# Token-major Fourier branch on half the spectrum, and modulation bursts issued 3000 instead of 400 places ahead

## The chip, the core and the metric

The kernel runs on one core of a Trainium2 chip. A core has TensorE (PE, matmuls into PSUM, 8 banks of 128 x 512 float32), VectorE (DVE), ScalarE (ACT), GpSimd (POOL) and SyncE (SP), which issues most of the transfers. The metric is the device time of one execution in microseconds; less is better. The time before is the median of 3 runs.

## What is computed

Two layers of a diffusion backbone over 256 latent and 256 context tokens, width 1024. A layer modulates and normalises its input, projects it, runs three mixers beside each other (latent attention "MLA", grouped attention "GQA", and a Fourier mixer), merges them with sigmoid gates, projects, and ends in a gated ConvFFN. The second layer computes only the latent tokens beyond the keys and values. The parts that the change touches are these:

```
mod = silu_c @ w_mod + b_mod                  # 1024 x 6144, for the latents and for the context
h = rms_norm(x, g) * (1 + scale) + shift      # scale and shift are parts of mod
f = (h @ w_in)[..., FOUR_START:GATE_START]    # 512 columns: 4 groups of 128

def fourier_mix(f):                           # per sample of 256 tokens
    z = fftn(f.reshape(b, l, 4, 128), axes=(tokens, channels of a group), norm="ortho")
    return real(z).reshape(b, l, 512)
y = ... + g_four * (fourier_mix(f) @ w_four)
```

For real input, the real part of the two-dimensional transform is C_tok f C_ch - S_tok f S_ch, with C and S the cosine and sine matrices over tokens and over channels. The order of the two transforms is free. The cosine part is even and the sine part odd in the token frequency, so that the frequencies 129 to 255 follow from 1 to 127.

## The kernel before

All matrix products are done as three matmuls (`mm3`, lines 104 to 106): each operand is split (`split`, lines 118 to 126) into a rounded high part on ScalarE and the rest on VectorE, and high x high, high x low and low x high are summed in one PSUM bank. Weights arrive by `wchunk` (line 89 issues the transfer on SP's queue) in pieces of 128 x 1024, three buffers deep, and are split too.

The kernel is written in an ordinary order: modulation of layer 0, norm, keys and values, GQA queries, the Fourier branch, GQA heads with gate and branch projections between them as fillers, latents, MLA heads with fillers, output projection, norm, FFN; then layer 1. A planner fixes each engine's order when the program is built: among the instructions that its own timeline shows ready it takes the one with the lowest rank, and the rank is the place in the ordinary order. `tc.high_priority(n)` moves the rank n places ahead. PSUM banks have names: "mm", "s" and "pt" have two buffers each, "o" and "tk" one each. On-chip tiles with one tag share its buffers in the same way.

Fourier branch (lines 554 to 600). `TQ` is 512 tokens in layer 0 (two samples, NS = 2) and 256 in layer 1. In each of two rounds `c` of 256 channels, the projection is made channel-major (`fp`: weights as the stationary operand, tokens moving, TQ columns); its result `f`, channels on partitions, is the stationary operand of the channel transform (`Y`: cosine and sine side by side, 256 columns for each of two groups), and `Y`, tokens on partitions, is that of the sequence transform (`Z`: four matmul triples for each group and sample, two token tiles x cosine and sine, 256 columns). Each of `fp`, `Y` and `Z` is split on its way to the next step. `load_dft` (line 1059) loads and splits five tables of 128 x 256; three of them hold tiles of the tag "pr", which the attention's softmax also uses.

Modulation bursts (`mod_burst`, line 235). A layer's 6 blocks of 1024 modulation columns are computed in bursts, a quarter of the reduction at a time: two transfers of 512 KB into the two buffers "mraw", 8 matmuls at line 254 that each use a strip of 32 columns of the array (the profile counts 16), and the sum into `row`. The fourth burst of a block ends with `turn`, two transposes in the same bank. Most bursts use the bank "tk". The bursts are placed as fillers between heads and FFN steps; their matmuls alone are moved ahead by MOD_AHEAD:

```
with tc.high_priority(MOD_AHEAD):
    for i in (1, 0):
        k = 2 * q + i
        for g in range(4):
            nc.tensor.matmul(ps[32 * g:32 * g + 32, :256], ...)
```

Of the kernel before, what the change touches and what calls it, by code (L numbers as in the profile page):

```python
# [8 lines left out]
F32 = mybir.dt.float32  # L9
F32R = mybir.dt.float32r  # L10
# [5 lines left out]
P = 128  # L16
D = 1024
KD = D // P
# [7 lines left out]
FOUR_START = 1440  # L26
# [4 lines left out]
RAWBUFS = 3  # L31
WBUFS = 3
RSQRT_MAGIC = 0x5F3759DF
MOD_AHEAD = 400


@with_exitstack
def hybrid_kernel(ctx: ExitStack, tc: tile.TileContext, a: dict, out: bass.AP):
    nc = tc.nc
# [5 lines left out]
    S = ctx.enter_context(tc.tile_pool(name="S", bufs=1))  # L45
# [8 lines left out]
    def pm(name, tag="mm"):  # L54
        return psum.tile([P, 512], F32, tag=tag, name=name, bufs=BANKS[tag])

    def pair(tag, name, bufs=None):

        return S.tile([P, 2, 512], F32R, tag=tag, name=name, bufs=bufs)
# [20 lines left out]
    def wchunk(W, k0, nk, c0, ncol, name):  # L80

        npc = -(-nk * ncol // WMAX)
        kpp = -(-nk // npc)
        parts = []
        for i in range(0, nk, kpp):
            kn = min(nk - i, kpp)
            n = kn * ncol
            raw = wpool.tile([P, WMAX], F32, tag="raw", name=f"{name}_w{i}", bufs=RAWBUFS)
            ins = nc.sync.dma_start(
                out=raw[:, :n].rearrange("p (k c) -> p k c", k=kn),  # L90
                in_=W[(k0 + i) * P:(k0 + i + kn) * P, c0:c0 + ncol].rearrange("(k p) c -> p k c", p=P))
            hi = wpool.tile([P, WMAX], F32R, tag="whi", name=f"{name}_h{i}", bufs=WBUFS)
            lo = wpool.tile([P, WMAX], F32R, tag="wlo", name=f"{name}_l{i}", bufs=WBUFS)
            split(raw[:, :n], hi[:, :n], lo[:, :n])
            parts.append((hi, lo))

        def w(k, c, m):
            j, r = divmod(k, kpp)
            return tuple(t[:, r * ncol + c:r * ncol + c + m] for t in parts[j])
        w.last = ins.ins  # L100
        return w
# [13 lines left out]
    def split(src, hi, lo, scale=None, later=False):  # L115

        if scale is None:
            nc.scalar.copy(hi, src)  # L118
        else:
            nc.scalar.activation(hi, src, AF.Copy if isinstance(scale, float) else AF.Identity, scale=scale)  # L120

        def low():
            if scale is None:
                nc.vector.tensor_sub(lo, src, f(hi))  # L124
            else:
                nc.vector.scalar_tensor_tensor(lo, src, scale, f(hi), op0=ALU.mult, op1=ALU.subtract)
        if later:
            return low
        low()
# [238 lines left out]
    def fm_group(w, cols, nk, xs, T, evac, name, tag="mm", whole=None):  # L368


        if T * len(cols) <= 512 and nk <= KD:
            ps = pm(f"{name}_0", tag)
            pss = [ps[:, i * T:(i + 1) * T] for i in range(len(cols))]
            order = [(k, i) for i in range(len(cols)) for k in range(nk)]
        else:
            pss = [pm(f"{name}_{i}", tag[i] if isinstance(tag, tuple) else tag) for i in range(len(cols))]
            order = [(k, i) for k in range(nk) for i in range(len(cols))]
        for k, i in order:
            wh, wl = w(k, cols[i], P)
            mm3(pss[i][:, :T], wh, wl, xs[k][:, 0, :T], xs[k][:, 1, :T], k == 0, k == nk - 1)  # L380
        if whole and T * len(cols) <= 512:
            whole(ps[:, :T * len(cols)])
            return
        rest = [evac(i, pss[i][:, :T]) for i in range(len(cols))]
        for r in rest:
            if callable(r):
                r()
# [19 lines left out]
    def layer(l, p, modT, last, xT, mods, prep, wkvg=None, norm=None):  # L407
        n_ = f"L{l}"
        TQ = 256 if last else 512
        NTQ = TQ // P  # L410
# [143 lines left out]
        of_ = []  # L554
        with after("qg0"):
            dft = load_dft(l)
        for c in range(2):
            w = wchunk(w_in, 0, KD, FOUR_START + c * 256, 256, f"{n_}fo{c}")
            if last:
                ft = S.tile([P, 2, 2, TQ], F32R, tag=f"D{2 * c}", name=f"{n_}f{c}")  # L560
                fs = [ft[:, i] for i in range(2)]
            else:
                fs = [pair(f"D{2 * c + i}", f"{n_}f{c}{i}") for i in range(2)]
            fm_group(w, [0, P], KD, hs, TQ,
                     lambda i, ps: split(ps, fs[i][:, 0, :TQ], fs[i][:, 1, :TQ], later=True), f"{n_}fp{c}", "mm" if c == 0 else "o" if last else ("o", "tk"),
                     whole=lambda ps: split(ps.rearrange("p (i t) -> p i t", i=2), ft[:, :, 0, :], ft[:, :, 1, :]))
            Y = []
            for tt in range(NTQ):
                ps = pm(f"{n_}Y{c}{tt}", "s")
                ts = slice(tt * P, (tt + 1) * P)  # L570
                for i in range(2):
                    mm3(ps[:, i * 256:(i + 1) * 256], fs[i][:, 0, ts], fs[i][:, 1, ts],
                        dft[0][:, 0, :], dft[0][:, 1, :], True, True)
                y = pair(f"X{tt}", f"{n_}Y{c}{tt}")
                split(ps, y[:, 0, :], y[:, 1, :])
                Y.append(y)
            if last:
                zp = pm(f"{n_}Z{c}", "pt")
                zps = [zp[:, :TQ], zp[:, TQ:]]
            for i in range(2):  # L580
                ps = zps[i] if last else pm(f"{n_}Z{c}{i}", "pt")
                for s in range(NS):
                    n = 0
                    for t2 in range(2):
                        for cs in range(2):
                            y = Y[s * 2 + t2]
                            wsl = slice(i * 256 + cs * P, i * 256 + (cs + 1) * P)
                            q = 1 + t2 * 2 + cs
                            mm3(ps[:, s * 256:(s + 1) * 256], y[:, 0, wsl], y[:, 1, wsl],
                                dft[q][:, 0, :], dft[q][:, 1, :], n == 0, n == 3)  # L590
                            n += 1
                if not last:
                    o = pair(f"B{2 * c + i}", f"{n_}fo{c}{i}")
                    split(ps, o[:, 0, :], o[:, 1, :])
                    of_.append(o)
            if last:
                op = S.tile([P, 2, 2, TQ], F32R, tag=f"B{c}", name=f"{n_}fo{c}")
                split(zp.rearrange("p (i t) -> p i t", i=2), op[:, :, 0, :], op[:, :, 1, :])
                of_ += [op[:, 0], op[:, 1]]
        gF, bF = merge(2, "w_four", of_, True)  # L600

        def attend(scores, vl, o_dst, odd, nm):
# [456 lines left out]
    def load_dft(l):  # L1059

        d4 = S.tile([P, 2, 2, 256], F32R, tag="D4", name=f"dft{l}d")
        ts = [d4[:, 0], d4[:, 1]] + [S.tile([P, 2, 256], F32R, tag="pr", name=f"dft{l}{i}", bufs=3) for i in range(3)]
        for i, t in enumerate(ts):
            if i == 0:
                src = a["dft_d"]
            else:
                t2, cs = divmod(i - 1, 2)
                src = a["dft_s"][t2 * P:(t2 + 1) * P, cs * 256:(cs + 1) * 256]
            raw = S.tile([P, 256], F32, tag="ot", name=f"dft{l}r{i}", bufs=2)
            nc.sync.dma_start(out=raw, in_=src)  # L1070
            nc.scalar.copy(t[:, 0, :], raw)
            nc.vector.tensor_sub(t[:, 1, :], raw, f(d4)[:, i, 0, :] if i < 2 else f(t)[:, 0, :])
        return ts
# [35 lines left out]
def _tables():  # L1109
    import numpy as np  # L1110

    def rope(rot_dim):
        n_f = rot_dim // 4
        t = np.arange(SEQ)
        row, col = (t // 64).astype(np.float32), (t % 64).astype(np.float32)
        inv = (np.float32(10000.0) ** (-np.arange(n_f, dtype=np.float32) / np.float32(n_f))).astype(np.float32)
        ang = np.concatenate([row[:, None] * inv, col[:, None] * inv], axis=-1).astype(np.float32)
        c, s = np.cos(ang, dtype=np.float32), np.sin(ang, dtype=np.float32)
        return np.concatenate([c, c, -s, s], axis=-1)

    rope_tab = np.concatenate([rope(32), rope(64)], axis=-1).astype(np.float32)

    def dft(n):
        k = np.arange(n)
        ang = 2.0 * np.pi * ((k[:, None] * k[None, :]) % n) / n
        return np.cos(ang) / np.sqrt(n), np.sin(ang) / np.sqrt(n)

    cd, sd = dft(128)
    cs, ss = dft(SEQ)
    return {  # L1130
        "rope_tab": np.ascontiguousarray(rope_tab),
        "dft_d": np.concatenate([cd, sd], axis=1).astype(np.float32),
        "dft_s": np.concatenate([cs, -ss], axis=1).astype(np.float32),
    }


# [25 lines left out]
```

## Time and profile before

| | |
|---|---|
| median of 3 runs | 1423.36 us (1422.74 to 1425.29) |
| the profiled execution | 1422.24 us |
| its span, first to last instruction | 1420.40 us |
| PE busy | 1379.5 us |
| DVE, ACT, POOL busy | 892.4, 662.2, 332.9 us |

The profiled execution's time is 1.84 us longer than its span and 1.12 us shorter than the median. Matmuls are pipelined: the length shown for one contains the time until its result has left the array, so the pace is read from start to start and not from the length. A line of a helper (104, 118, 124) serves many places; there the tile's name says which.

### The profile page before, as it was taken

To read this page: it belongs to the slowest core of one execution; us is meant where nothing else is said; L and a number is where in the kernel's file an instruction comes from. 1 tells how busy PE (TensorE), PEld (TensorE's weight loads), DVE (VectorE), ACT (ScalarE), POOL (GpSimd) and SP (SyncE) were. 2 spreads that over 40 slices of the span, in tenths; PEclk is the share of its full clock that TensorE was granted. 3 is DMA by queue.
4 is the path that set the end of the run, shared out by engine and by line. 5 is a ranking of instruction groups with operands and counts; after the bars stand their busy time and mean duration, and the time that the engine had idled before them with its cause. 6 is when DMAs were issued, how large, how long until landed. Compare 5 with 4: busy or idle time off the path is not lost.

```text
span 1420.4 us, 23006 instructions
## 1 busy us (share of the span) xinstructions
PE 1379.5 (97%) x8801; PEld 1195.3 (84%) x8801; DVE 892.4 (63%) x1644; ACT 662.2 (47%) x1164; POOL 332.9 (23%) x399
## 2 busy tenths in 40 slices
PE   6999999999999999999999999999998998999998
PEld 4988888878888788878678888899977998899998
DVE  5575655666645666655326663677687766788853
ACT  4434545435554344444114442445564663566642
POOL 3211323364323311101000111121245332112200
PEclk9999999999999999999999999999999999999999
DMA  9733442143321745343343232363744555466663
GB/s 318 247 89 105 148 146 73 54 120 106 90 74 38 262 149 197 101 148 104 104 134 91 87 99 91 111 177 95 229 134 140 155 176 188 129 180 186 184 191 121
DMA packets 163064, 197.97 MB, mean 139 GB/s; under 512 B 7144, under 2 KB 149530, under 8 KB 162954
## 3 DMA queue, kind: packets, MB, share of 16 engines
q1 hardware_dynamic: 161952, 195.85, 44.5%
q0 software_dynamic: 864, 0.61, 0.4%
q8 instruction: 69, 1.13, 0.3%
q14 instruction: 41, 0.34, 0.1%
q10 hardware_dynamic: 138, 0.04, 0.0%
HBM read 192.28 MB, written 3.15 MB: 138 GB/s over the span
## 4 chain that ended last, share of the span: by engine, by line
PE 89%; DVE 5%; DMA 2%; POOL 1%; issue 1%; ACT 1%; SPq 1%; DVEq 0%; ACTq 0%; POOLq 0%
PE L0upp L104 6%; PE L0upp L105 6%; PE L0upp L106 6%; PE mod_ps L254 3%; PE L1upp L104 3%; PE L1upp L105 3%; PE L1upp L106 3%; PE L0dp L106 3%; PE L0dp L104 3%; PE L0dp L105 3%; PE L0gp L106 3%; PE L0gp L104 3%; PE L0gp L105 3%; PE L1dp L106 1%; PE L1dp L104 1%; PE L1dp L105 1%
## 5 line engine op out<-in xcount | busy, mean ns | idle before, releaser
L104 PE MATMUL L0upp<-L0n_h,L0up_h 128*128 128x512 f32 (+1 forms) x384 | 141.7, 373 | 1.1 <-ACT L0n_h L332 1.1
L105 PE MATMUL L0upp<-L0n_h,L0up_h 128*128 128x512 f32 (+1 forms) x384 | 141.9, 373 | 0.0
L106 PE MATMUL L0upp<-L0n_h,L0up_l 128*128 128x512 f32 (+1 forms) x384 | 140.0, 373 | 0.0
L984 POOL TENSOR_TENSOR L0sg<-L0sg,L0u 128x512 f32<-128x512 f32 x22 | 31.4, 1426 | 288.6 <-DVE L0u L961 274.9
L104 PE MATMUL L1upp<-L1n_h,L1up_h 128*128 128x256 f32 x352 | 96.5, 286 | 1.1 <-ACT L1n_h L332 1.1
L106 PE MATMUL L1upp<-L1n_h,L1up_l 128*128 128x256 f32 x352 | 97.0, 285 | 0.0
L105 PE MATMUL L1upp<-L1n_h,L1up_h 128*128 128x256 f32 x352 | 96.4, 285 | 0.0
L124 DVE TENSOR_TENSOR L0up_l<-L0up_w,L0up_h 128x1024 fp32r<-128x1024 f32 x44 | 58.8, 1337 | 53.7 <-ACT L0up_h L118 50.6
L104 PEld LDWEIGHTS L0upp<-L0n_h,L0up_h 128*128 128x128 f32 x384 | 71.8, 188 | 15.4 <-issue 1.6
L106 PEld LDWEIGHTS L0upp<-L0n_h,L0up_l 128*128 128x128 f32 x384 | 72.1, 188 | 13.6 <-issue 0.8
L105 PEld LDWEIGHTS L0upp<-L0n_h,L0up_h 128*128 128x128 f32 x384 | 72.0, 188 | 13.5 <-issue 0.8
L118 ACT CAST L0up_h<-L0up_w 128x1024 fp32r<-128x1024 f32 x44 | 46.3, 1053 | 72.2 <-PE L0upp L105 49.7
L104 PE MATMUL L0gp<-L0n_h,L0g_h 128*128 128x512 f32 x192 | 76.3, 397 | 0.0
L105 PE MATMUL L0gp<-L0n_h,L0g_h 128*128 128x512 f32 x192 | 75.5, 393 | 0.0
L106 PE MATMUL L0gp<-L0n_h,L0g_l 128*128 128x512 f32 x192 | 75.2, 396 | 0.1
L106 PE MATMUL L0dp<-L0act,L0dn_l 128*128 128x512 f32 (+1 forms) x196 | 72.7, 371 | 0.0
L104 PE MATMUL L0dp<-L0act,L0dn_h 128*128 128x512 f32 (+1 forms) x196 | 72.6, 370 | 0.0
L105 PE MATMUL L0dp<-L0act,L0dn_h 128*128 128x512 f32 (+1 forms) x196 | 72.5, 370 | 0.0
L104 PEld LDWEIGHTS L1upp<-L1n_h,L1up_h 128*128 128x128 f32 x352 | 66.9, 194 | 1.5 <-ACT L1n_h L332 1.5
L106 PEld LDWEIGHTS L1upp<-L1n_h,L1up_l 128*128 128x128 f32 x352 | 67.3, 194 | 0.0
L105 PEld LDWEIGHTS L1upp<-L1n_h,L1up_h 128*128 128x128 f32 x352 | 66.8, 194 | 0.0
L124 DVE TENSOR_TENSOR L1up_l<-L1up_w,L1up_h 128x1024 fp32r<-128x1024 f32 x44 | 54.2, 1231 | 18.6 <-ACT L1up_h L118 17.2
(1534 smaller groups left out, 4322.9 us busy)
## 6 DMA issues: line engine op xcount, KB each, us to landing
mod_w<-in_w_mod_dram SPq DMA_DIRECT2D x96, 512.0 KB, 5.0
L0up_w<-in_w_up_dram SPq DMA_DIRECT2D x44, 512.0 KB, 3.6
L1up_w<-in_w_up_dram SPq DMA_DIRECT2D x44, 512.0 KB, 4.3
L0g_w<-in_w_in_dram SPq DMA_DIRECT2D x24, 512.0 KB, 3.7
L1g_w<-in_w_in_dram SPq DMA_DIRECT2D x24, 512.0 KB, 4.0
L0dn_w<-in_w_down_dram SPq DMA_DIRECT2D x20, 512.0 KB, 3.5
L1dn_w<-in_w_down_dram SPq DMA_DIRECT2D x16, 512.0 KB, 3.5
L0wo_w<-in_w_o_dram SPq DMA_DIRECT2D x8, 512.0 KB, 7.0
```

What stands on the lines that cost most here:

```text
L104: nc.tensor.matmul(ps, lh, rh, start=start, stop=False)
L105: nc.tensor.matmul(ps, lh, rl, start=False, stop=False)
L106: last_mm[0] = nc.tensor.matmul(ps, ll, rh, start=False, stop=stop).ins
L118: nc.scalar.copy(hi, src)
L124: nc.vector.tensor_sub(lo, src, f(hi))
L254: nc.tensor.matmul(ps[32 * g:32 * g + 32, :256], cpad[:, 2 * k:2 * k + 32], raws[i][:, g * 256:(g + 1) * 256], start=i == 1, stop=i == 0, ...
L984: nc.gpsimd.tensor_mul(g[:, :TQ], g[:, :TQ], us[1][:, :TQ])
```

## The change

The Fourier branch is made token-major: the projection takes the tokens as the stationary operand and 512 channels as the moving one; its result, tokens on partitions, goes into the sequence transform first (`A`: 129 cosine and 127 sine frequencies side by side, 256 columns), and that into the channel transform, with the table as the stationary operand: `zc` (cosine, 2 x 130 columns) and `zs` (sine, 2 x 128). The frequencies 0 to 128 of `z` are the sum and 129 to 255 the difference, written in reverse order, of the two. Two of the five tables are gone. MOD_AHEAD goes from 400 to 3000.

```diff
-MOD_AHEAD = 400
+MOD_AHEAD = 3000
...
-        for c in range(2):
-            w = wchunk(w_in, 0, KD, FOUR_START + c * 256, 256, f"{n_}fo{c}")
...
-            fm_group(w, [0, P], KD, hs, TQ, ...)
-            Y = []
-            for tt in range(NTQ):
-                ps = pm(f"{n_}Y{c}{tt}", "s")
...
-            for i in range(2):
-                ps = zps[i] if last else pm(f"{n_}Z{c}{i}", "pt")
-                for s in range(NS):
...
+        w = wchunk(w_in, 0, KD, FOUR_START, 512, f"{n_}fo")
+        pss = [pm(f"{n_}fp{tt}", ("mm", "s")[tt // 2]) for tt in range(NTQ)]
+        for k0 in range(0, KD, 2):
+            for tt in range(NTQ):
+                ts = slice(tt * P, (tt + 1) * P)
+                for k in (k0, k0 + 1):
+                    wh, wl = w(k, 0, 512)
+                    mm3(pss[tt], hs[k][:, 0, ts], hs[k][:, 1, ts], wh, wl, k == 0, k == KD - 1)
+        ft = [pair(f"D{tt}", f"{n_}f{tt}") for tt in range(NTQ)]
+        for tt in range(NTQ):
+            split(pss[tt], ft[tt][:, 0, :], ft[tt][:, 1, :])
+
+        nb = 2 * NS
+        pss = [pm(f"{n_}A{b}", ("pt", "pt", "o", "tk")[b] if not last else "s") for b in range(nb)]
+        for s in range(NS):
+            for g in range(4):
+                b, hf = (g, s) if NS == 2 else divmod(g, 2)
+                gs = slice(g * P, (g + 1) * P)
+                for t2 in range(2):
+                    f_ = ft[s * 2 + t2]
+                    mm3(pss[b][:, hf * 256:(hf + 1) * 256], f_[:, 0, gs], f_[:, 1, gs],
+                        dft[1 + t2][:, 0, :], dft[1 + t2][:, 1, :], t2 == 0, t2 == 1)
+        As = [pair(f"X{b}", f"{n_}A{b}") for b in range(nb)]
+        for b in range(nb):
+            split(pss[b], As[b][:, 0, :], As[b][:, 1, :])
+        for b in range(nb):
+            ah, al = (As[b][:, i, :].rearrange("p (s k) -> p s k", s=2) for i in range(2))
+            zc = pm(f"{n_}Zc{b}", "mm" if not last else "pt")[:, :260].rearrange("p (s k) -> p s k", s=2)
+            zs = pm(f"{n_}Zs{b}", "s" if not last else ("o", "tk")[b])[:, :256].rearrange("p (s k) -> p s k", s=2)
+            mm3(zs, dft[0][:, 0, P:], dft[0][:, 1, P:], ah[:, :, P:], al[:, :, P:], True, True)
+            mm3(zc, dft[0][:, 0, :P], dft[0][:, 1, :P], ah[:, :, :130], al[:, :, :130], True, True)
+            zt = S.tile([P, 256], F32, tag="ot", name=f"{n_}zt{b}", bufs=2).rearrange("p (s k) -> p s k", s=2)
+            nc.scalar.copy(zt, zs)
+            z = S.tile([P, 512], F32, tag="pr", name=f"{n_}z{b}", bufs=3)
+            z3 = z.rearrange("p (s k) -> p s k", s=2)
+            nc.vector.tensor_add(z3[:, :, 1:P], zc[:, :, 1:P], zt[:, :, 1:])
+            nc.vector.tensor_sub(z3[:, :, 255:P:-1], zc[:, :, 1:P], zt[:, :, 1:])
+            nc.scalar.copy(z3[:, :, 0:P + 1:P], zc[:, :, 0:P + 1:P])
...
+                o = pair(f"B{b}", f"{n_}fo{b}")
+                split(z, o[:, 0, :], o[:, 1, :])
+                of_.append(o)
...
-        ts = [d4[:, 0], d4[:, 1]] + [S.tile([P, 2, 256], F32R, tag="pr", name=f"dft{l}{i}", bufs=3) for i in range(3)]
+        ts = [d4[:, 0], d4[:, 1], S.tile([P, 2, 256], F32R, tag="pr", name=f"dft{l}", bufs=3)]
...
-        "dft_s": np.concatenate([cs, -ss], axis=1).astype(np.float32),
+        "dft_s": np.concatenate([cs[:, :129], -ss[:, 1:128]], axis=1).astype(np.float32),
```

## Rows read from the trace of the kernel before

**Rows 1.** The page: busy time per engine, and the chain by engine.

```profile
PE 1379.5 (97%) x8801; PEld 1195.3 (84%) x8801; DVE 892.4 (63%) x1644; ACT 662.2 (47%) x1164; POOL 332.9 (23%) x399
...
PE 89%; DVE 5%; DMA 2%; POOL 1%; issue 1%; ACT 1%; SPq 1%; DVEq 0%; ACTq 0%; POOLq 0%
```

**Rows 2.** Windows: stretch, length, busy PE, PEld, DVE, ACT, POOL, clock, DMA.

```profile
71.00:117.00 46.00, 46.00 (x276) 41.10 (x275) 31.77 (x63) 17.39 (x27) 5.86 (x11) 1.00 0.28 81
941.00:975.00 34.00, 34.00 (x243) 31.99 (x242) 25.28 (x54) 16.18 (x24) 5.26 (x11) 1.00 0.46 130
1050.00:1090.00 40.00, 32.60 (x230) 28.65 (x229) 34.83 (x74) 22.23 (x41) 24.17 (x25) 0.99 0.55 163
```

**Rows 3.** Timeline of PE in layer 0's Fourier stage: start, length, instruction.

```profile
72.04 0.39 PE L106 MATMUL L0fp<-L0n_h,L0fo_l 128*128 128x512 f32 x1
...
85.64 0.39 PE L106 MATMUL L0fp<-L0n_h,L0fo_l 128*128 128x512 f32 x1
...
110.85 0.28 PE L104 MATMUL L0Z<-dft,L0Y 128*128 128x256 f32 x1
...
111.81 0.28 PE L106 MATMUL L0Z<-dft,L0Y 128*128 128x256 f32 x1
```

**Rows 4.** Windows by tile: L0fp, L0Y, L1fp, L1Y; busy PE (count), PEld, DVE, ACT.

```profile
66.00:125.00 59.00, 22.49 (x96) 17.76 (x96) 2.73 (x4) 2.34 (x4) 1.00 0.23 65
...
66.00:125.00 59.00, 18.70 (x144) 18.19 (x144) 5.34 (x8) 4.60 (x8) 1.00 0.23 65
...
935.00:980.00 45.00, 11.85 (x96) 11.66 (x96) 1.36 (x2) 1.17 (x2) 1.00 0.46 130
...
935.00:980.00 45.00, 9.50 (x72) 9.16 (x72) 2.67 (x4) 2.25 (x4) 1.00 0.46 130
```

**Rows 5.** Instructions by tile, L0Y and mod_ps: ns min/median/max, first and last start.

```profile
L118 ACT CAST L0Y<-L0Y x8: 587/588/591, 89.9 to 110.9; 128x512 fp32r<-128x512 f32 x8
L124 DVE TENSOR_TENSOR L0Y<-L0Y,L0Y x8: 680/691/693, 90.5 to 111.6; 128x512 fp32r<-128x512 f32 x8
...
L261 DVE TENSOR_TENSOR mod_row<-mod_row,mod_ps x30: 394/420/422, 132.2 to 1219.2; 128x256 f32<-128x256 f32 x30
...
L258 ACT COPY mod_row<-mod_ps x10: 353/372/390, 124.6 to 1215.9; 128x256 f32<-128x256 f32 x10
```

**Rows 6.** Timeline of PE around a modulation burst at 617 us.

```profile
617.05 0.39 PE L106 MATMUL L0upp<-L0n_h,L0up_l 128*128 128x512 f32 x1
617.37 1.07 PE L254 MATMUL mod_ps<-mod_w,cpad 128*32 128x256 f32 x16
...
618.71 0.40 PE L105 MATMUL L0upp<-L0n_h,L0up_h 128*128 128x512 f32 x1
```

**Rows 7.** Timeline of PE around two other bursts, 657 to 684 and 706 to 714 us.

```profile
657.21 0.39 PE L105 MATMUL L0upp<-L0n_h,L0up_h 128*128 128x512 f32 x1
...
658.42 0.39 PE L104 MATMUL L0upp<-L0n_h,L0up_h 128*128 128x512 f32 x1
...
676.58 0.39 PE L105 MATMUL L0dp<-L0act,L0dn_h 128*128 128x512 f32 x1
...
684.10 0.39 PE L106 MATMUL L0dp<-L0act,L0dn_l 128*128 128x512 f32 x1
...
705.87 0.39 PE L106 MATMUL L0dp<-L0act,L0dn_l 128*128 128x512 f32 x1
706.19 0.62 PE L254 MATMUL mod_ps<-mod_w,cpad 128*32 128x256 f32 x2
...
714.37 0.39 PE L105 MATMUL L0dp<-L0act,L0dn_h 128*128 128x512 f32 x1
```

**Rows 8.** Chain in order of time and SP's timeline: two bursts and the loads between.

```profile
122.90 1.00 PE mod_ps L254 x16
...
130.87 1.00 PE mod_ps L254 x16
...
123.53 0.81 SPq L248 DMA_DIRECT2D mod_w<-in_w_mod_dram  x2
```

More of the change, by code (lines that the diff above doesn't have):

```diff
@@ L559, in layer @@
             if last:
-                ft = S.tile([P, 2, 2, TQ], F32R, tag=f"D{2 * c}", name=f"{n_}f{c}")
-                fs = [ft[:, i] for i in range(2)]
-            else:
[L563 to L566, printed above, removed]
@@ L567, in layer @@
-            Y = []
-            for tt in range(NTQ):
-                ps = pm(f"{n_}Y{c}{tt}", "s")
-                ts = slice(tt * P, (tt + 1) * P)
-                for i in range(2):
[L572 to L579, printed above, removed]
@@ L580, in layer @@
-            for i in range(2):
-                ps = zps[i] if last else pm(f"{n_}Z{c}{i}", "pt")
-                for s in range(NS):
[L583 to L599, printed above, removed]
+                op = S.tile([P, 2, 2, TQ], F32R, tag=f"B{b}", name=f"{n_}fo{b}")
+                split(z3, op[:, :, 0, :], op[:, :, 1, :])
+                of_ += [op[:, 0], op[:, 1]]
+            else:
+                o = pair(f"B{b}", f"{n_}fo{b}")
+                split(z, o[:, 0, :], o[:, 1, :])
+                of_.append(o)
@@ L1066, in load_dft @@
             else:
-                t2, cs = divmod(i - 1, 2)
-                src = a["dft_s"][t2 * P:(t2 + 1) * P, cs * 256:(cs + 1) * 256]
+                src = a["dft_s"][(i - 1) * P:i * P, :]
             raw = S.tile([P, 256], F32, tag="ot", name=f"dft{l}r{i}", bufs=2)
```

## The prediction

> **What bounds the kernel now.** I read the page first: TensorE is busy 97% of the span, VectorE 63%, and 89% of the chain that ended last is TensorE time [rows 1]. 40.9 us of the 1420.4 us are without a matmul. So a microsecond of matmuls removed should be about a microsecond gained, unless the removed piece stood in a stage that waits for something else. I checked that by stretches [rows 2]: through both layers' Fourier stages TensorE is busy without a break (46.00 of 46, 34.00 of 34) while VectorE has room (31.77 and 25.28). In layer 1 a later stretch is different: from 1050 to 1090 TensorE does 32.60 of 40 and VectorE 34.83.
>
> Then the pace of the matmuls, from the starts in the timeline, since their shown lengths overlap [rows 3]: from 72.04 to 85.64 lie 60 starts of 512 columns, 0.2267 us each; from 110.85 to 111.81 lie 8 starts of 256 columns, 0.120 us each. Last, the modulation bursts, one by one [rows 5 to 7].
>
> **Change, part 1: Fourier matmuls.** The counts by tile [rows 4] agree with the code. Layer 0 now: 96 projection matmuls of 512 columns, and 144 of 256 that read or write Y (48 for the channel transform, 96 for the sequence transform). After: the projection is 8 k x 4 token tiles x 3 = 96 of 512 columns, the same; the sequence transform 2 samples x 4 groups x 2 token tiles x 3 = 48 of 256; the channel transform 4 tiles x 2 x 3 = 24 of 256 or 260. 144 become 72: 72 x 0.120 = 8.64 us less. 260 columns against 256 adds under 2% of 12 matmuls, nothing.
> Layer 1 now: 96 of 256 columns for the projection and 72 on Y, 168 x 0.120 = 20.16 us. After: 8 x 2 x 3 = 48 of 512, 24 and 12 of 256: 48 x 0.2267 + 36 x 0.120 = 15.20. 4.96 us less.
>
> **Part 2: what the other engines do.** A split of 512 columns takes 0.587 us on ScalarE and 0.690 on VectorE; 256 columns read from PSUM take VectorE 0.42 and ScalarE 0.37 [rows 5]. Layer 0 had 16 splits; it gets 12 splits and, for each of 4 tiles, an add, a subtract and two copies. VectorE: 16 x 0.690 = 11.0 becomes 12 x 0.690 + 8 x 0.42 = 11.6; ScalarE 9.4 becomes 8.5 to 10.0, as the two-column copy is near nothing or near 0.37. Layer 1: 8 splits (5.5) become 6 and 4 adds (5.8). The reversed write of the subtract has no row: below, the plain 0.42; above, I allow 0.69. Two of five DFT loads go in each layer, each with a split shorter than those rows. Together this is within 1 us of nothing on engines with room [rows 2], hidden by the matmuls; uncovered it appears in part 4. Weights arrive in pieces of the same size; a piece now feeds 12 matmuls of 512 columns in layer 1 (2.72 us) where it fed 24 of 256 (2.88): at most 4 x 0.16 = 0.6 us of waiting, I take none.
>
> **Part 3: the modulation bursts.** A burst is 8 matmuls (16 in the trace) on four 32-column strips. Issued in one piece it costs little: from the start at 617.05 to that at 618.71 are 1.66 us, of which two normal intervals are 0.45, so 1.21 us [rows 6]. Two of the 40 bursts are not in one piece: their pairs stand one by one between down-projection matmuls. The second takes 705.87 to 714.37 with 11 normal intervals (2.49): 8.50 - 2.49 = 6.01 us. The first has one pair at 657 (1.21 - 0.45 = 0.76) and seven from 676.58 to 684.10 (7.52 - 10 x 0.2267 = 5.25): 6.01 us again [rows 7]. One burst matmul and one ordinary matmul alternate: I read this as two runs of equal rank, the burst moved ahead by 400 and the ordinary order at that place, merged by the planner. Moved ahead by 3000 they would meet no equal: their data is not loaded that early, so they should go out in one piece when it is. 2 x (6.01 - 1.21) = 9.6 us less. Bounds: 0 if they stay threaded, 9.6. I take 9.6, as 38 of 40 bursts are in one piece.
> For those 38 I expect nothing. The first burst ends after 122.90, the load for the next is issued at 123.53 and its matmuls stand at 130.87 [rows 8]: buffers, loads and the one "tk" bank time them, not the rank. A burst's loads keep their ordinary place on SP's queue, behind the weights; if bursts run earlier, so do the loads that wait for their two buffers.
>
> **Part 4: new waits.** All four projection accumulators now close in the last weight piece, 6 x 0.2267 = 1.36 us apart, and the channel transform turns over two "mm" and two "s" banks for four tiles. After the sequence transform's last matmul, VectorE needs 0.587 + 0.690 for the last split and 0.84 for the first add and subtract: a bank is free at 2.12 us, while two tiles give TensorE 2 x 0.72 = 1.44. So 0.68 of waiting, then 0.12 and 0.84 for the next turns: 1.6 us. Behind these matmuls wait the gate group (same "mm" banks) and the first head's scores ("s"); the key transposes can fill. I take 2.0 in layer 0. In layer 1 the latent projection is ready and needs other banks by then: 0.5. Bounds: 0 below; above, every turn in series, 1.28 + 1.28 + 4 x 1.53 = 8.7 in layer 0 and 1.28 + 1.28 + 2 x 1.53 = 5.6 in layer 1, 14.3 together. I choose 2.5, near the lower end, because the same kinds of split ended 16 times in layer 0's stage without one gap [rows 2].
> The Trainium skill speaks against the change here: "Perfetto Trace Analysis", section "Matmuls", wants independent groups to rotate through different PSUM banks so that emptying one overlaps the next group. By that rule the turns would lie open and the saving would shrink by the 14.3; the full TensorE rows of that stage are against so much.
> Layer 1's stretch at 1050 to 1090 [rows 2] may swallow part of layer 1's gain, as VectorE's work before it does not shrink: 0 to 4.96; I take 1.5, since the matmuls that feed this stretch come earlier too.
>
> **Sum.** -8.64 - 4.96 - 9.60 + 2.5 + 1.5 = -19.2 us. The profiled execution took 1422.24 us (span 1420.40 and 1.84 around it): 1403.0. The median of the runs is 1.12 above it: 1404. With 0.2% (2.8 us) about what a measurement of this kernel can tell from no change, this is clearly faster.
>
> **Rivals.** (a) The bursts stay threaded, or thread elsewhere: -9.6 us is missing, 1414. For it: the planner's ranks aren't in the trace. Against: 38 whole bursts.
> (b) The turns of part 4 lie open, also by the skill's rule: 2.5 becomes 14.3, 1416. For it: two banks for four tiles. Against: gate and key work is at hand.
> (a) and (b) together: 9.6 + 11.8 of the 19.2 are gone; that ends at 1425.6, no change.
> (c) Slower: bursts so far ahead take the one "tk" bank, and the fourth burst of a block keeps it until its transposes, which keep their ordinary place. Heads that need "tk" for their transposes then wait for a gate group, 48 x 0.2267 = 10.9 us. Five blocks run beside attention; from two holds uncovered on (21.8) it is no gain, with three (32.6) 1437. Against it: burst and bank already alternate by data and buffers [rows 8]. For it: one bank, and the distance.
> (d) Better: no new wait, and fuller TensorE later; 23.2 or more less, below 1400.
>
> **How the numbers follow.** Chances: the forecast (1398 to 1409) 0.50, (a) 0.14, (b) 0.13, both 0.06, (c) 0.07, (d) 0.10. Faster by over 0.2%: 0.50 + 0.14 + 0.13 + 0.10 = 0.87; within: 0.06; slower: 0.07. The range 1396 to 1417 takes in the forecast, (a), (b) and half of (d), 0.82.
>
> **What the profile will show.** TensorE busy time lower by some 20 us; no mod_ps piece "x2" near 650 to 715; 72 matmuls of 256 columns in layer 0's Fourier stage, its TensorE gaps under 3 us; attention waits for "tk" not longer. I am wrong if TensorE gets new gaps of over 10 us in all, if bursts thread in other places, or if layer 1's end moves less than its start.

## The result, and the profile after

The median falls from 1423.98 us (1422.74 to 1425.29, 4 runs) to 1407.06 us (1404.73 to 1411.13, 4 runs): ratio 0.9884, 95% interval 0.9855 to 0.9913, that is 16.5 us less (12.4 to 20.6). The forecast was 1404, in a range of 1396 to 1417. The profiled execution after took 1404.73 us, its span is 1403.0, 17.4 below that of before. One execution on record, of a kernel of experiment 6, took 4798 us with each of its stretches 2.9 to 3.6 times as long, and no number here uses it.

The page after, busy time by engine and the chain; it answers to [rows 1]:

```profile
PE 1359.2 (97%) x8645; PEld 1180.0 (84%) x8645; DVE 889.1 (63%) x1646; ACT 660.0 (47%) x1166; POOL 336.2 (24%) x399
...
PE 89%; DVE 5%; DMA 2%; ACT 1%; POOL 1%; issue 1%; SPq 0%; DVEq 0%; ACTq 0%; POOLq 0%
```

TensorE does 20.3 us less and still bounds the kernel. A span cannot be judged by its length alone here. I cut it at instructions that every version has, and list the time from the first of one tile to the first of the next (A: L0fp to L0o, layer 0's Fourier branch and attention; B: L0upp to L1kvg, layer 0's FFN; C: L1fp to L1m0tk, the first key transposes of layer 1's latent heads; D: L1fp to L1o, of which C is the first part; the rest is what is left of the span, the same code in all versions but for the loads and splits of the DFT tables, two fewer in a layer with the new branch):

| profile | A | B | C | D | rest |
|---|---|---|---|---|---|
| before | 393.7 | 387.8 | 123.9 | 240.9 | 398.0 |
| after | 387.6 | 378.2 | 123.9 | 243.0 | 394.2 |
| difference | -6.1 | -9.6 | 0.0 | +2.1 | -3.8 |

So in this pair of profiles layer 0's Fourier branch gave 6.1 us, the bursts 9.6, layer 1's Fourier branch cost 2.1, and 3.8 came from the rest, where the change touches only the table loads. The experiments below show that of these the 9.6 repeats best, to within 0.6.

**The bursts.** TensorE's timeline after, the places of the two bursts of [rows 7]:

```profile
633.49 0.39 PE L105 MATMUL L0upp<-L0n_h,L0up_h 128*128 128x512 f32 x1
633.81 1.07 PE L254 MATMUL mod_ps<-mod_w,cpad 128*32 128x256 f32 x16
634.81 0.51 PE L106 MATMUL L0upp<-L0n_h,L0up_l 128*128 128x512 f32 x1
635.15 0.40 PE L104 MATMUL L0upp<-L0n_h,L0up_h 128*128 128x512 f32 x1
...
643.01 1.07 PE L254 MATMUL mod_ps<-mod_w,cpad 128*32 128x256 f32 x16
```

Both stand whole now, earlier than before and among the up-projection's matmuls. From 633.49 to 635.15 are 1.66 us, as in [rows 6].

**Layer 0's Fourier stage.** The counts of the tiles (one line of three for the projection, one of six for the sequence transform with its two tables, one of six for the channel transform, whose other three are L0Zs):

```profile
L104 PE MATMUL L0fp<-L0fo_h,L0n_h x32: 389/389/397, 73.5 to 94.6; 128*128 128x512 f32 x32
...
L104 PE MATMUL L0A<-dft,L0f x8: 283/283/284, 96.3 to 100.6; 128*128 128x256 f32 x8
...
L104 PE MATMUL L0Zc<-L0A,dft0d x4: 284/336/391, 101.1 to 107.4; 128*128 128x260 f32 x4
```

L0fp has 96 matmuls as before, and the 144 of 256 columns became 72. Windows of after: the layer-0 stage from the first L0fp to the first gate matmul, and in layer 1 from the first L1fp to the first gate matmul. Before, such stretches had no gap in layer 0 [rows 2] and 0.2 us in layer 1 (41.50 of 41.70).

```profile
73.50:107.90 34.40, 31.79 (x173) 27.41 (x173) 27.76 (x61) 14.37 (x27) 4.61 (x9) 1.00 0.33 92
925.30:965.10 39.80, 37.11 (x221) 32.57 (x219) 31.47 (x73) 20.46 (x33) 7.12 (x14) 1.00 0.44 124
```

Each now has 2.6 to 2.7 us without a matmul. In layer 0 it is one gap; TensorE's timeline and then ScalarE's at that place, after:

```profile
104.54 0.28 PE L106 MATMUL L0Zc<-L0A,dft0d 128*128 128x260 f32 x1
107.43 0.39 PE L104 MATMUL L0Zc<-L0A,dft0d 128*128 128x260 f32 x1 [2.61 <-ACT L0z L595]
```

```profile
104.84 0.58 ACT L798 CAST L0KG<-L0gk 64x512 fp32r<-64x512 f32 x1
105.42 0.58 ACT L799 CAST L0KG<-L0gk 64x512 fp32r<-64x512 f32 x1
106.01 0.58 ACT L798 CAST L0KG<-L0gk 64x512 fp32r<-64x512 f32 x1
106.60 0.58 ACT L799 CAST L0KG<-L0gk 64x512 fp32r<-64x512 f32 x1
107.21 0.17 ACT L595 COPY L0z<-L0Zc 128x4 f32<-128x4 f32 x1
```

The fourth tile's cosine matmuls need the "mm" bank of the second one. That bank's last reader is the two-column copy of line 595, 0.17 us long, and it stands on ScalarE behind four key copies of 0.58 us. The Trainium skill, "PSUM — Partial Sum Buffer", section "Engine vs sequencer instructions", calls ScalarE's and VectorE's queues strictly first in, first out; the trace agrees, the copy starts 0.03 us after the last key copy ends. VectorE's last read of that bank, the subtract of line 594, had ended at 104.5 us. The key copies empty the key transposes that stood at 103.61, the very filler that the prediction had counted on.

**Layer 1.** The waits of TensorE from 925 to 1017 us, after:

```profile
PE L1cq L104 <- DVE L1ck L126: 1.2, 1, 1.2
PE L1A L106 <- DVE L1f L124: 1.1, 1, 1.1
PE L1gp L104 <- DVE L1rkv_y L141: 0.4, 1, 0.4
```

The second is the turn from the projection to the sequence transform, which needs both token tiles split; the first is the latent projection, which comes earlier and now waits for VectorE. And then the first key transposes, before and after; for after also what stands ahead of them: the copies and squares of the keys, their sums (line 736), the first and the last of the nine steps of the root (lines 136 to 144) and the scaling (tiles L1ktok, L1SK and L1rk_y; shortest, median and longest in ns, first and last start):

```profile
L867 PE MATMUL L1m0tk<-ident,L1ktok x4: 270/314/315, 1065.3 to 1068.3; 128*96 128x128 f32 x4
```

```profile
L729 ACT COPY L1ktok<-L1ukv x8: 362/366/392, 1019.5 to 1037.2; 128x256 f32<-128x256 f32 x8
L734 POOL TENSOR_TENSOR L1kq<-L1ktok x8: 612/612/927, 1030.0 to 1038.5; 128x256 f32<-128x256 f32 x8
L736 DVE TENSOR_REDUCE L1SK<-L1kq x8: 399/402/420, 1031.2 to 1040.7; 128x4 f32<-128x256 f32 x8
...
L136 DVE TENSOR_SCALAR L1rk_y<-L1SK x1: 180/180/180, 1041.4 to 1041.4; 128x32 int32<-128x32 int32 x1
...
L144 DVE SCALAR_TENSOR_TENSOR L1rk_y<-L1rk_t,L1rk_y x1: 964/964/964, 1047.0 to 1047.0; 128x32 f32<-128x32 f32 x1
L746 DVE TENSOR_TENSOR L1ktok<-L1ktok,L1rk_y x4: 693/1097/1105, 1048.0 to 1050.6; 128x512 f32<-128x512 f32 x4
...
L871 PE MATMUL L1m0tk<-ident,L1ktok x4: 314/314/316, 1049.2 to 1052.3; 128*96 128x128 f32 x4
```

With L1fp's first matmul at 941.4 before and 925.3 after, both are 123.9 us later. Whatever layer 1's Fourier branch saves is used up there, in the chain of key squares (POOL), their sums and root (VectorE) and the scaling; experiment 6 tests it. The nine steps of the root have 0.2 to 1.0 us each, 2.7 in all, and take from 1041.4 to 1047.9, because other instructions of VectorE stand between them; before they took from 1059.0 to 1062.4.

### The profile page after: what moved, and what is told of

Same layout as the page of the kernel before. It is cut to its first block, busy times and chain, and to the rows that moved or that the text cites. A ratio compares the mean times of both kernels' runs of the same rounds, so it can differ in the third digit from the quotient of the medians.

```text
span 1403.0 us, 22692 instructions
## 1 busy us (share of the span) xinstructions
PE 1359.2 (97%) x8645; PEld 1180.0 (84%) x8645; DVE 889.1 (63%) x1646; ACT 660.0 (47%) x1166; POOL 336.2 (24%) x399
## 4 chain that ended last, share of the span: by engine, by line
PE 89%; DVE 5%; DMA 2%; ACT 1%; POOL 1%; issue 1%; SPq 0%; DVEq 0%; ACTq 0%; POOLq 0%
PE L0upp L104 6%; PE L0upp L105 6%; PE L0upp L106 6%; PE L1upp L104 3%; PE L1upp L105 3%; PE L1upp L106 3%; PE L0dp L104 3%; PE L0dp L106 3%; PE L0dp L105 3%; PE L0gp L106 3%; PE L0gp L105 3%; PE L0gp L104 3%; PE mod_ps L254 3%; PE L1gp L106 2%; PE L1gp L104 2%; PE L1gp L105 2%
```

## Experiments

Ratios are to the kernel before on the same chip, with 95% intervals; microseconds that go with them are of 1424. The stretches A to D are those above.

**1. The order alone, the branch alone, and a whole burst in its old place.** The first is the kernel before with one line changed, the second the changed kernel with it changed back:

```diff
-MOD_AHEAD = 400
+MOD_AHEAD = 3000
```

> The kernel before with the larger issue offset (3000) alone; the Fourier branch is the old one. My theory (the two threaded bursts each cost 6.01 us and a whole one 1.21): 9.6 us faster than before, about 1414.4, with all of the difference between the second and the third layer-0 key projection's end and the first burst of layer 1. Rival (all of the gain is the Fourier branch's): no difference, 1424. Rival (the gain is larger, since the Fourier gain is partly given back): 12 us or more faster.

> The changed kernel with the old offset (400): the new Fourier branch alone. My theory: two bursts are threaded again and cost 9.6 us, so about 1416.6 against 1407 for the whole change, which is 7.4 us under the kernel before. Rival (the order is worth nothing): as the whole change, 1407.

The third keeps 400 and the old branch, and gives the eight matmuls of a burst one rank, each one place more ahead than the last:

```diff
-        with tc.high_priority(MOD_AHEAD):
-            for i in (1, 0):
-                k = 2 * q + i
-                for g in range(4):
+        for n, (i, g) in enumerate([(i, g) for i in (1, 0) for g in range(4)]):
+            k = 2 * q + i
+            with tc.high_priority(MOD_AHEAD + n):
...
```

> The kernel before, with all eight matmuls of a burst given one rank at the old offset, so that the two bursts that were threaded stay where they were, among the down-projection's matmuls, but stand (nearly) whole. If each break of the ordinary matmul stream by a single burst matmul is what costs ((6.01 - 1.21)/7 = 0.69 us a break): 8.9 to 9.6 us faster than before, about 1414.5 to 1415. If the place is what costs (a burst among the down-projection is dear, one ahead of it is not): no difference, 1424.

Measured: order alone 0.9941 (0.992 to 0.9961), 8.4 us less; branch alone 0.9961 (0.9946 to 0.9976), 5.6 us less; whole in the old place 0.9946 (0.993 to 0.9962), 7.7 us less. The windows of stretch B, one for each of the three kernels in this order:

```profile
519.40:897.70 378.30, 378.23 (x1934) 313.33 (x1935) 208.22 (x300) 143.35 (x196) 42.43 (x36) 1.00 0.37 119
```

```profile
515.90:903.70 387.80, 387.80 (x1935) 314.44 (x1935) 208.44 (x300) 143.54 (x196) 42.42 (x36) 1.00 0.36 117
```

```profile
521.40:900.40 379.00, 378.98 (x1935) 313.36 (x1935) 208.81 (x300) 143.53 (x196) 42.43 (x36) 1.00 0.37 119
```

TensorE is busy without a break in all three, with the same number of matmuls; only their order differs, and it is worth 9.5 us. In the third kernel the bursts stand where they stood in [rows 7], the first with one matmul ahead of the other seven, the second whole:

```profile
658.64 0.62 PE L253 MATMUL mod_ps<-mod_w,cpad 128*32 128x256 f32 x2
...
677.55 1.06 PE L253 MATMUL mod_ps<-mod_w,cpad 128*32 128x256 f32 x14
...
703.29 1.07 PE L253 MATMUL mod_ps<-mod_w,cpad 128*32 128x256 f32 x16
```

B has one piece more than after and is 0.8 us longer; 8.8 of the 9.6 us are gained. It is the breaks that cost and not the place. Order and branch add up: 8.4 + 5.6 = 14.0, inside the interval of the whole change.

**2. More breaks.** The changed kernel with an offset of 100. A smaller offset threads more: the planned order has 79 pieces of bursts where the changed kernel has 37.

```diff
-MOD_AHEAD = 3000
+MOD_AHEAD = 100
```

> The changed kernel with a smaller offset (100): 42 more pieces of bursts stand singly among other matmuls (79 groups in place of 37). If a break costs 0.69 us wherever it is: 29 us slower than the whole change, about 1436. If the cost belongs to the down-projection of layer 0 alone (where the two threaded bursts stood): 9.6 us slower, about 1417. If only a few of the breaks cost, because the matrix engine waits for something else in most of those places: in between.

Measured: 1.0101 (1.0086 to 1.0116) against 0.9884, 30.9 us slower than the whole change. The window of stretch B:

```profile
521.20:921.50 400.30, 400.28 (x1934) 315.76 (x1935) 208.77 (x300) 143.58 (x196) 40.70 (x36) 1.00 0.36 114
```

Of the 42 extra pieces 33 stand in B, which is 22.1 us longer than after: 0.67 us each. Five stand in A (+4.6 us), four in D (+2.1). All three together are 28.8 us for 42 pieces, 0.69 each, the price that [rows 6, 7] give.

**3. The copy that came late.** The changed kernel, one line, which serves both layers:

```diff
-            nc.scalar.copy(z3[:, :, 0:P + 1:P], zc[:, :, 0:P + 1:P])
+            nc.vector.tensor_copy(z3[:, :, 0:P + 1:P], zc[:, :, 0:P + 1:P])
```

> The changed kernel with the two-column copy of the layer-0 odd half on VectorE instead of ScalarE, where it stood behind four key-projection copies of about 0.58 us. Theory (ScalarE's order holds the psum bank and so the fourth tile's odd matmuls, which waited 2.6 us): the wait at the fourth tile goes, 2 to 2.6 us faster than the whole change, about 1404.5. Rival (the bank is late by VectorE's own additions, or the next tile waits as long for something else): no difference, 1407.

Measured: 0.9882 (0.9862 to 0.9903), by its time no different from the whole change. The trace tells more. TensorE's only wait in the stage, and the window of it:

```profile
PE L0gp L104 <- DVE L0z L595: 0.3, 1, 0.3
```

```profile
71.20:103.50 32.30, 31.86 (x174) 27.40 (x172) 26.86 (x63) 12.24 (x20) 4.61 (x9) 1.00 0.33 98
```

The 2.6 us gap is gone, and the stage takes 32.3 us instead of 34.4. Five profiles with this edit have a stretch A of 385.7 to 387.5 (mean 386.7), three with the new branch and without this edit, that of experiment 2 left out, 387.6 to 389.7 (388.8): 2.1 us, too little for the times to show. So ScalarE's order held the bank.

**4. One layer at a time.** The larger offset, and the new branch in one layer only; the old code stands in the other, with its five tables. The first kernel, the second has `if not last`:

```diff
+        if last:
+            for c in range(2):
+                w = wchunk(w_in, 0, KD, FOUR_START + c * 256, 256, f"{n_}fo{c}")
...
+        else:
+            w = wchunk(w_in, 0, KD, FOUR_START, 512, f"{n_}fo")
```

> The larger offset with the new Fourier branch in layer 0 alone (the old one in layer 1). Against the kernel before: 9.6 us from the bursts and 5.4 to 6.6 us from layer 0, so about 1408 to 1409; against the whole change it is 1 to 4.5 us slower if the layer-1 stage gave what its matmuls say, the same if the layer-1 gain is given back later in the layer.

> The larger offset with the new Fourier branch in layer 1 alone (the old one in layer 0). Theory (the layer-1 gain of about 5 us is mostly given back where the q tokens are waited for): 9.6 us from the bursts and 1 to 4.5 us from layer 1, so about 1410 to 1413.5. Rival (nothing is left of it): 1414.4.

Measured: layer 0 only 0.9884 (0.9869 to 0.9899), 16.5 us less, as the whole change; layer 1 only 0.9907 (0.9891 to 0.9923), 13.2 us less, which is 4.8 below the order alone. The first says that layer 1 is worth nothing, the second that it is worth nearly its matmuls. The stretches decide:

| profile | A | C | D | rest |
|---|---|---|---|---|
| order alone | 392.4 | 123.9 | 241.1 | 396.1 |
| branch alone | 389.2 | 123.9 | 243.1 | 392.9 |
| whole in the old place | 393.8 | 124.2 | 241.7 | 396.9 |
| copy on VectorE | 385.7 | 123.8 | 242.0 | 393.7 |
| layer 0 only | 389.7 | 123.9 | 241.4 | 395.3 |
| layer 1 only | 393.6 | 123.9 | 242.5 | 395.0 |

C is the same with either branch. D is 240.7 to 241.7 with the old branch (five profiles, with the one of the next experiment; mean 241.1) and 242.0 to 243.1 with the new one (four; mean 242.6): the new branch is 1.5 us slower there. The output projection behind it (L1o to L1upp, the same code) takes 36.8 to 40.1 us with the old and 34.6 to 39.9 with the new, less where the granted clock was higher (last section). From L1fp to L1upp it is then 278.2 to 281.7 (mean 280.2) against 277.2 to 281.9 (279.7). So by the stretches layer 1's branch changes the time by something between 0.5 us less and 1.5 us more. That the two measured times differ by what else varies is the reading left, and is not shown apart.

**5. Layer 0 only, with the copy on VectorE.** The version that the runs so far point to:

> Larger offset, new Fourier branch in layer 0 alone with its two-column copy on VectorE, old branch in layer 1. In all runs so far the first key transposes of layer 1's latent heads start 123.8 to 124.6 us after that layer's first Fourier matmul, with either branch. Theory (layer 1's gain is wholly used up by then): 0 to 2 us faster than the kernel with both new branches and the copy on VectorE (1404.34), so about 1403. Rival (the new branch in layer 1 is worth its matmuls): 3 to 5 us slower than that kernel, about 1408.

Measured: 0.9868 (0.9849 to 0.9887), 1404.09 us, the lowest of the kernels that leave nothing out, and not to be told from the whole change (0.9884) or from that with the copy (0.9882). Its stretches are 387.2, 378.2, 123.9 and 240.7. The rival's 3 to 5 us are excluded, the gain of 0 to 2 us isn't shown.

**6. What sets the key transposes of layer 1.** Three kernels with the copy on VectorE, one of them run twice. In the first the value subtraction of line 730 stands twice in layer 1:

```diff
+                    if last:
+                        nc.vector.scalar_tensor_tensor(VM[tt][:, h4, 1, :], v4[:, :, 64:128], rkv[:, tt:tt + 1],
+                                                       f(VM[tt])[:, h4, 0, :], op0=ALU.mult, op1=ALU.subtract)
```

> The kernel with both new branches and the copy on VectorE, with the 8 value subtractions of layer 1 (0.48 us each on VectorE) made twice. Theory (VectorE's backlog from the latent projections to the key tokens sets the first latent head): that head's first key transposes come 3 to 3.8 us later, 127 to 128 us after the layer's first Fourier matmul, and the kernel is 2 to 4 us slower. Rival (a transfer or TensorE sets it): 123.8 again, no difference.

In the others the sums are left out, with the new and with the old branch in layer 1:

```diff
+        if last:
+            nc.vector.memset(SK[:, :NK], 64.0)
...
-                    nc.vector.reduce_sum(SK[:, s0:s0 + 4], sq4, axis=AX.X)
+                    if not last:
+                        nc.vector.reduce_sum(SK[:, s0:s0 + 4], sq4, axis=AX.X)
```

> The kernel with both new branches and the copy on VectorE, where layer 1's 8 sums of squares of the keys (0.33 us each on VectorE) are left out and a constant stands in their place. Theory (VectorE sets the first latent head): the key transposes come 1.5 to 2.6 us earlier, 121.2 to 122.3 us after the layer's first Fourier matmul. Rival: 123.8 again.

> The same 8 sums left out, with the old branch in layer 1. Theory (VectorE alone limits the stretch): as with the new branch, 121.2 to 122.3 us after the layer's first Fourier matmul, no difference between the two branches. Rival (in the old branch TensorE limits the stretch too): 123 to 124 us with the old branch, so that the new one is ahead by 1 to 2 us once VectorE is relieved.

> The kernel without layer 1's 8 sums of squares, with both new branches, once more, for its profile (of the first one the only profile is of an execution of 4798 us, the others were 1390 to 1398). With the old branch in layer 1 the first key transposes came 113.2 us after that layer's first Fourier matmul, 10.6 earlier than with the sums, where I had expected 1.5 to 2.6. If the wait for the sums of squares hid the gain of the new branch: 110.5 to 111.5 here, 2 to 2.5 us ahead of the old one. If something else that both branches share sets it: 113.2.

Measured: more work 0.9892 (0.9875 to 0.9909), not to be told from 0.9882; without the sums 0.9807 (0.9781 to 0.9832) with the new branch and 0.98 (0.9782 to 0.9818) with the old; the repeat, one run, 1393.07 us beside 1422.91. The profile of the kernel without the sums and with the new branch is the repeat's. Windows of stretch C: with more work, without the sums and with the new branch (the repeat), and without the sums with the old one:

```profile
927.20:1053.40 126.20, 120.03 (x854) 105.73 (x853) 98.56 (x216) 72.22 (x138) 35.48 (x46) 1.00 0.52 158
```

```profile
923.70:1035.70 112.00, 108.69 (x786) 95.80 (x785) 84.78 (x189) 62.47 (x120) 32.51 (x42) 1.00 0.52 159
```

```profile
922.80:1036.00 113.20, 112.98 (x869) 102.34 (x869) 84.21 (x185) 62.37 (x120) 30.46 (x42) 1.00 0.52 157
```

3.8 us more on VectorE moved the transposes by 2.4, less than I expected. It moved the last L1ukv matmul by 2.6 (113.2 instead of 110.6 us after the first L1fp) and not the chain behind it (13.0 instead of 13.2 us). Leaving out 8 sums of 0.40 us each moved the transposes by 10.6 to 11.7, where 1.5 to 2.6 was expected: my theory of a VectorE that is simply full was too small. With the sums the transposes start 13.2 us after the last L1ukv matmul (1036.0 to 1049.2 after; 10.8 us before), without them 0.7 us after it in both kernels. So what hangs on the sums, the chain of squares, sums and root, whose short steps stand in queues between the splits, is the length of that wait. Without the sums the new branch is 1.2 us ahead at the last L1ukv matmul (111.4 against 112.6), still 1.2 at the transposes (112.0 against 113.3) and 0.4 at the end of stretch D (235.6 against 236.0): between the two cases that I had set, with one profile of each. With the sums 2.3 us reached that matmul and nothing was left at the transposes. So the chain takes what reaches it; why only 1.2 us reach it without the sums, these runs don't show.

## Why the prediction came out, and where it did not

**The matmuls removed (8.64 and 4.96): right in count, TensorE's busy time falls by 20.3 us with the bursts.** The three terms add up to 23.2; the difference is not traced. Fewer matmuls were less time only where no other engine set the next step.

**The threaded bursts (9.6): right in cause, and in size to within 0.6.** B is shorter by 9.6 us in this pair; it is 387.8 in both profiles at offset 400 with the planner's order, 378.2 to 378.8 in all nine at 3000. Experiments 1 and 2 show cause and price. Rival (a), that they stay threaded, fell with the profile after.

**Layer 0's new waits (2.0 of the 2.5): near the size, the wrong cause.** I had three bank turns of 0.68, 0.12 and 0.84 us, from VectorE's add and subtract. The trace has one wait of 2.6 us, for a 0.17 us copy that I had costed as "near nothing or near 0.37" and never placed in ScalarE's order. Stretch A with the old branch is 392.4 to 393.8 (four profiles, mean 393.4), with the new one 388.8: 4.6 us gained where 6.6 were forecast. Experiment 3 gives 2.1 back. The 8.64 less this wait would leave 6.0; where the other 1.4 went no run here shows.

**Rival (b), open turns, 14.3: fell.** The Trainium skill, "Perfetto Trace Analysis", section "Matmuls", asks for independent groups to rotate through different banks. Two banks for four tiles did cost something, so the rule has a point; but with the copy on VectorE 0.3 us of waiting is left with the same two banks, so here the late reader was enough to make the wait; whether more banks would have hidden it, no run here shows.

**Layer 1 (-4.96 + 0.5 + 1.5, so 3.0 gained): the step that failed.** The new waits are 2.3 us inside the stage (1.1 for the split of f, 1.2 for the latent's split), not 0.5: I had filled the turn with a latent projection that was itself waiting for VectorE. The other 2.3 to 2.4 us are still there at the last L1ukv matmul and gone at the key transposes. I allowed up to 4.96 for this stretch and took 1.5. All of it went, and by the output projection the branch is 1.5 us behind. The loss behind the transposes goes with more idle time of TensorE and a lower granted clock. From the first key transposes to L1o, before and after (third number from the end the clock):

```profile
1065.20:1182.30 117.10, 111.11 (x892) 103.79 (x892) 84.27 (x142) 65.80 (x121) 46.21 (x45) 0.99 0.55 172
1049.20:1168.30 119.10, 111.38 (x878) 103.83 (x878) 83.89 (x143) 65.21 (x119) 46.05 (x44) 0.96 0.52 165
```

In the five profiles with the old branch TensorE is without a matmul for 5.7 to 6.1 us there, at a mean clock of 0.97 to 0.99; in the four with the new one for 7.0 to 7.7, at 0.96 to 0.97, and it is busy as long with some 14 fewer matmuls. What makes it wait longer, and whether the output projection really gives that back, isn't settled.

**Rival (c), the "tk" bank held: fell.** With the order alone A, C and D differ from before by -1.3, 0.0 and +0.2 us. **Rival (d), below 1400: fell too**, the lowest of the four runs is 1404.73.

**The sum.** By mean stretches it should have been -4.6 - 9.6 and -0.5 to +1.5 for layer 1, together -12.7 to -14.7 us; the forecast had -19.2 and the times have -16.5 (12.4 to 20.6 less). The 1404 was thus nearer than its working deserves: in the profile after, 3.8 us came from the rest, and most of that went with the granted clock (last section). That part is luck. Of the signs that I named, TensorE's fall, the missing single pieces, the 72 matmuls and gaps under 3 us came true. Layer 1's end did move more than its start (17.4 against 13.1), which I had taken as a sign of being right, and stretch D shows that it isn't one here.

## What to carry to other kernels

Price a removed matmul only up to the next thing that TensorE waits for: cut the traces of before and after at the same instructions and look whether the saved time is still there behind that wait. When an edit gives a bank a new last reader, however short, look at what stands before that reader in its engine's queue. And where matmuls of different shapes are mixed by a planner, compare the planned orders, for with the same matmuls on a TensorE that never rests, order alone was 9.5 us.

## What the hardware showed that I had not expected

**A break has much the same price each time.** Between matmuls of 128 x 128, each further piece into which a burst on 32-column strips is broken costs 0.69 us, in two bursts (14 extra pieces, 9.6 us) as in 42 extra pieces (28.8 us), though eight matmuls in a row take 1.21 us in all. What in the array takes it, no run here shows.

**Unchanged code varied by some microseconds.** Up to the first L0fp, TensorE's order is the same in the kernels compared here, yet that matmul starts between 70.9 and 74.0 us in the profiles. The stretch of 20 to 36 us, before and after, with the clock third from the end:

```profile
20.00:36.00 16.00, 12.30 (x114) 7.56 (x118) 10.61 (x32) 7.55 (x17) 1.47 (x2) 1.00 1.09 348
```

```profile
20.00:36.00 16.00, 13.20 (x100) 7.91 (x92) 8.28 (x23) 6.21 (x14) 0.00 (x0) 0.77 1.09 348
```

After had the lower clock there, part of the time at 1.2 instead of 2.4 GHz, and started its Fourier stage 2.6 us later. It was the other way round in layer 1's output projection (L1o to L1upp): 40.0 us at a mean clock of 0.91 before, 36.8 at 0.95 after, and 34.6 at 1.00 with the new branch in layer 1 only. Three windows of before, the 4 us at the start of that stretch, in which TensorE is without a matmul for 2.5 us, and the 8 behind them, in which the clock falls; then the whole stretch of the last kernel:

```profile
1182.30:1186.30 4.00, 1.48 (x11) 1.10 (x10) 4.00 (x5) 1.58 (x3) 2.35 (x1) 1.00 0.39 129
1186.30:1190.30 4.00, 3.02 (x15) 2.32 (x16) 4.00 (x8) 0.80 (x3) 1.39 (x1) 0.77 0.45 134
1190.30:1194.30 4.00, 4.00 (x20) 4.00 (x20) 0.29 (x1) 0.00 (x0) 0.00 (x0) 0.50 0.44 131
```

```profile
1176.70:1211.30 34.60, 30.70 (x276) 27.32 (x274) 23.31 (x46) 14.60 (x24) 8.23 (x7) 1.00 0.52 163
```

The same 276 matmuls take 33.83 or 30.70 us of TensorE. The stretch from L1kvg to L1fp is alike: it takes 30.2 to 30.9 us in the six profiles in which its mean clock is 1.00, after among them, and 32.3 to 33.3 in the four with 0.89 or 0.90, before among them. Such stretches are the "rest" of the tables, and their differences are as large as what layer 1's branch could have given.
